# Seven products in place of eight for 18 of the second layer's 22 pairs of up-projection tiles, with neighbouring pairs interleaved

## The chip, the cores and the metric

The kernel runs on one core of a Trainium2 chip. The metric is the device time of one execution in microseconds (us); lower is better. Engines are named as the profile names them: PE (TensorE, matmuls), PEld (its weight loads), DVE (VectorE), ACT (ScalarE), POOL (GpSimd), SP (SyncE, which here only issues DMAs).

## What is computed

A two-layer encoder trunk runs over 768 tokens: 512 of a prompt and 256 of a sample, which share the weights but not the conditioning vector. Each layer has a mixer (attention and convolution) and then a gated feed-forward block (FFN). The change lies in the FFN of the second layer:

```python
D_MODEL = 1024
D_FF = 2816

def conv_ffn(h, w_up, dw_w, w_down):
    a, g = jnp.split(h @ w_up, 2, axis=-1)
    g = depthwise_conv(g, dw_w)          # width 3, centred, per request
    return (a * jax.nn.gelu(g)) @ w_down

def trunk(...):
    for l in range(DEPTH):
        ...
        h = rms_norm(x, norm2_g[l]) * (1 + s2) + sh2
        x = x + g2 * conv_ffn(h, w_up[l], ffn_dw_w[l], w_down[l])
```

## The kernel before

Everything lies transposed, 128 features on the partitions and 768 tokens along the free axis. The tokens form two groups, 512 and 256 wide (`GROUPS`). The precision comes from split numbers: a float32 value is kept as a high part `hi` (rounded) and a low part `lo` (the rest), and one product is three matmuls, `wl*xh`, `wh*xl`, `wh*xh` (`three`, L349 to L352).

Weights arrive as tiles of 128 x 1024 numbers (512 KB), eight blocks of 128 columns each. One list, `stream`, sets their order for the whole kernel. SP loads tile after tile into a ring of `RAW` = 5 buffers (L233); `consume` (L306) splits each one: ACT writes `wh` (L324), ACT writes `wl` = -raw (L328), and a DMA issued by POOL adds raw to it in place (L329), so that `wl` ends as raw minus its rounded part. The ring of split tiles has `PAIRS` = 4 places. `unit` hands the next split tile to a product.

The kernel is written in the order of a planner with its own clock: `tick` (L120) counts the matmuls' time, starts work that falls due (`after`), and lets `feed` (L332) split the next tile when at least 1.3 us of that clock have passed since the last and a place in the ring is free. The planner only sets the order in which instructions are written. On the chip every engine takes its own instructions in that order, and each instruction waits for what it reads and for the place that it writes.

The FFN of a layer (`ffn`, L856) works through 22 pairs f = 0 to 21. Pair f has two up-projection tiles, a and g, of 128 features each over all 1024 inputs: `product` (L358) runs 24 matmuls of 512 columns and 24 of 256 for each tile. `hidden` (L859) then makes the pair's hidden features: the convolution of g (ACT L865, DVE L866 and L867), GELU (ACT L868), the product with a (DVE L869), and the split of the result (ACT L870, POOL L871). The pairs are grouped by `CHUNKS` = (4, 4, 4, 4, 2, 4). `part` (L447) multiplies a finished group's hidden features by the down-projection, one weight tile per pair, and DVE adds the result to x (L445). It runs once per group, behind the first pair of the next group; the last two groups are multiplied at the end.

Names in what follows: `h_k` is the FFN's input (block k of 8, high and low), `a`, `g` the results of the two tiles in PSUM (eight banks), `gc` the hidden features on their way, `pd` the down-projection's results.

## Time and profile before

| | |
|---|---|
| median of 3 runs | 1901.63 us (1891.21 to 1901.82) |
| the profiled execution | 1892.81 us, of which the span from first to last instruction is 1891.0 us |
| mean granted TensorE clock | 0.991 of full speed |
| PE busy | 1840.4 us, 97% of the span |
| second layer's FFN | from about 1338 us to the end |

The page's first part gives each engine's busy time. Its slices (40 of them, 47.3 us each) show in tenths how busy an engine is along the span, and PEclk the clock that PE was granted. A row of the timeline has the start, the duration, the engine, the line and the operation with the tiles that it writes and reads; in brackets stands idle time in front of it and what ended it. Matmuls are pipelined, so that a matmul's time is the distance from its start to the next start, not its duration.

### The profile page before, as it was taken

What the parts mean: (1) busy time and instruction counts of PE and PEld (TensorE: products, weight loads), DVE (VectorE), ACT (ScalarE), POOL (GpSimd) and SP (SyncE); (2) the same over time, 40 slices, a digit from 0 to 9 for tenths busy, and PEclk for the clock granted to TensorE, in tenths of its full rate; (3) what the DMA queues carried; (4) which work ended last, traced back from release to release, by engine and by line L of the source; (5) the groups of instructions that cost most, each with busy time, mean ns of one, the idle gap of its engine ahead of it and who ended that gap; (6) DMA issues with size and microseconds to landing.
All of it is one profiled execution on the core that took longest, in us unless ns stands there. A gap on an engine that the chain in (4) does not pass through costs nothing.

```text
span 1891.0 us, 27649 instructions
## 1 busy us (share of the span) xinstructions
PE 1840.4 (97%) x11164; PEld 1552.1 (82%) x11164; DVE 1000.3 (53%) x1779; ACT 816.8 (43%) x1315; POOL 367.4 (19%) x344
## 2 busy tenths in 40 slices
PE   6999999999999999999999999999899999999999
PEld 4789676778888888888878986768788888888888
DVE  6667666776655655664367886666622221313123
ACT  3324667554423242433343357675543333333331
POOL 1103110033211121211232131100521121211110
PEclk9999999999999999999999999999999999999999
DMA  9666431236667777685635542223457464646454
GB/s 339 176 174 192 122 90 44 67 90 162 184 191 199 212 183 212 156 228 147 145 86 127 124 119 64 65 59 97 93 131 162 106 148 112 149 100 151 101 122 112
DMA packets 80913, 261.81 MB, mean 138 GB/s; under 512 B 9137, under 2 KB 18609, under 8 KB 80785
## 3 DMA queue, kind: packets, MB, share of 16 engines
q0 software_dynamic: 26640, 97.01, 28.4%
q1 hardware_dynamic: 54144, 163.03, 25.4%
q8 instruction: 88, 1.44, 0.3%
q14 instruction: 41, 0.33, 0.1%
HBM read 159.83 MB, written 3.18 MB: 86 GB/s over the span
## 4 chain that ended last, share of the span: by engine, by line
PE 90%; DVE 3%; ACT 2%; issue 2%; DMA 2%; POOL 1%; SPq 0%; POOLq 0%; ACTq 0%; DVEq 0%
PE a L351 6%; PE g L351 6%; PE g L352 6%; PE a L352 6%; PE a L350 6%; PE g L350 6%; PE pd L351 5%; PE pd L352 5%; PE pd L350 5%; PE s L729 4%; PE tp L763 2%; PE o L774 2%; PE v L350 1%; DMA wl<-raw 1%; PE q L350 1%
## 5 line engine op out<-in xcount | busy, mean ns | idle before, releaser
L329 POOL DMA_DIRECT2D wl<-raw x185 | 163.9, 886 | 691.1 <-ACT wl L328 498.0
L324 ACT ACTIVATE wh<-raw 128x1024 fp32r<-128x1024 f32 x188 | 197.2, 1049 | 163.4 <-PE pd L352 69.1
L866 DVE SCALAR_TENSOR_TENSOR gc<-g,fw_sb,gc 128x511 f32<-128x511 f32 x84 | 51.4, 612 | 389.6 <-ACT gc L865 389.6
L558 DVE SCALAR_TENSOR_TENSOR acc<-up,cw_sb,acc 128x783 f32<-128x783 f32 x240 | 246.8, 1028 | 4.3
L328 ACT ACTIVATE wl<-raw 128x1024 fp32r<-128x1024 f32 x185 | 193.4, 1046 | 0.0
L351 PE MATMUL pd<-hl,wh 128*128 128x512 f32 (+1 forms) x576 | 193.2, 335 | 0.0
L352 PE MATMUL pd<-hh,wh 128*128 128x512 f32 (+1 forms) x576 | 192.8, 335 | 0.0
L350 PE MATMUL pd<-hh,wl 128*128 128x512 f32 (+1 forms) x576 | 192.4, 334 | 0.0
L871 POOL TENSOR_TENSOR hl<-gc,hh 128x768 fp32r<-128x768 f32 x44 | 81.8, 1860 | 543.5 <-ACT hh L870 543.5
L865 ACT ACTIVATE gc<-g,fw_sb 128x512 f32<-128x512 f32 x84 | 48.2, 573 | 305.6 <-PE g L352 305.6
L292 DVE CUSTOM_DVE_ANT_0 cro<-raw,cr 128x1024 f32<-128x1024 f32 x112 | 166.6, 1488 | 4.2 <-ACT cr L285 1.5
L445 DVE SCALAR_TENSOR_TENSOR x<-pd,mod,x 128x512 f32<-128x512 f32 (+1 forms) x160 | 96.3, 615 | 133.9 <-PE pd L352 133.9
L350 PEld LDWEIGHTS pd<-hh,wl 128*128 128x128 f32 x576 | 108.1, 188 | 12.3
L351 PEld LDWEIGHTS pd<-hl,wh 128*128 128x128 f32 x576 | 108.3, 188 | 11.7
L352 PEld LDWEIGHTS pd<-hh,wh 128*128 128x128 f32 x576 | 108.2, 188 | 11.4
L868 ACT ACTIVATE gc<-gc 128x512 f32<-128x512 f32 x88 | 46.2, 525 | 130.1 <-DVE gc L867 130.1
L729 PE MATMUL s<-kT,qT 64*128 64x512 f32 (+1 forms) x192 | 94.1, 570 | 0.0
L869 DVE TENSOR_TENSOR gc<-a,gc 128x512 f32<-128x512 f32 x84 | 46.9, 558 | 55.0 <-ACT gc L868 55.0
L741 ACT ACTIVATE sp<-sp,nm 128x512 f32<-128x512 f32 (+1 forms) x96 | 62.1, 647 | 27.5 <-DVE nm L739 24.6
L739 DVE CUSTOM_DVE_ANT_0 sp<-s,G 128x512 f32<-128x512 f32 (+1 forms) x96 | 57.1, 596 | 24.0 <-PE s L729 24.0
L750 ACT ACTIVATE sp<-sp,den 128x512 f32<-128x512 f32 (+1 forms) x96 | 61.8, 645 | 9.0 <-DVE den L748 8.8
L764 ACT ACTIVATE PT<-tp 128x512 f32<-128x512 f32 (+1 forms) x96 | 49.3, 518 | 22.5 <-PE tp L763 21.9
(697 smaller groups left out, 5165.2 us busy)
## 6 DMA issues: line engine op xcount, KB each, us to landing
wl<-raw POOLq DMA_DIRECT2D x185, 512.0 KB, 5.8
raw<-in_w_up SPq DMA_DIRECT2D x88, 512.0 KB, 4.7
raw<-in_wadaT SPq DMA_DIRECT2D x48, 512.0 KB, 5.7
raw<-in_w_down SPq DMA_DIRECT2D x44, 512.0 KB, 4.5
raw<-in_w_in SPq DMA_DIRECT2D x40, 512.0 KB, 4.7
raw<-in_wada SPq DMA_DIRECT2D x24, 512.0 KB, 7.0
raw<-in_w_out SPq DMA_DIRECT2D x16, 512.0 KB, 4.7
G<-bt SPq DMA_DIRECT2D x16, 448.0 KB, 4.5
```

Of the source, the lines that this page charges most:

```text
L292: nc.vector.tensor_tensor_reduce(out=rows["out"], in0=r, in1=rows[g], op0=ALU.mult, op1=ALU.add, scale=1.0, scalar=0.0, accum_out=mod[l][: ...
L324: nc.scalar.activation(hi, r, AF.Copy)
L328: nc.scalar.activation(lo, r, AF.Copy, scale=-1.0)
L329: nc.gpsimd.dma_start(out=lo, in_=r, accum_op=ALU.add)
L350: nc.tensor.matmul(ps, wl, xh, start=first, stop=False)
L351: nc.tensor.matmul(ps, wh, xl, start=False, stop=False)
L352: nc.tensor.matmul(ps, wh, xh, start=False, stop=last)
L445: nc.vector.scalar_tensor_tensor(x[ot][:, span(g)], ps, mod[l][:, gate + ot, g:g + 1], x[ot][:, span(g)], op0=ALU.mult, op1=ALU.add)
L558: nc.vector.scalar_tensor_tensor(a, up[i][:, t:t + ACW], K["cw"][:, l, i, t:t + 1], a, op0=ALU.mult, op1=ALU.add)
L729: nc.tensor.matmul(ps[:, :w], qT[hp][64 * s:64 * s + 64, o + i * P:o + (i + 1) * P], kT[hp][64 * s:64 * s + 64, o:o + w], start=True, stop ...
L741: nc.scalar.activation(sp[:, :w], sp[:, :w], AF.Exp, scale=-1.0, bias=nm, accum_out=den)
L871: nc.gpsimd.tensor_tensor(lo, gc, hi.bitcast(F32), op=ALU.subtract)
```

## The change

For 18 pairs of the second layer (f = 4 to 21, all groups but the first, `SEVEN`), a pair's two up-projections become seven products of half size. The 1024 inputs are cut into two halves of four blocks, the tokens into two halves of 384 (`HALF`), and the pair's two tiles a and g are the two columns of a 2 x 2 arrangement of blocks. Strassen's scheme (in Winograd's form) then needs seven block products, each of four blocks and 384 tokens: 12 matmuls of 384 columns. The products take sums and differences as operands:

- Weights (a1, a2 the halves of tile a, g1, g2 those of tile g): A is tile a itself (split as before, its low part by the DMA); S holds g1+g2 and g1+g2-a1 (`sums`); B is g2 (`last_block`); R holds a1-g1 and a2-(g1+g2-a1) (`differences`). DVE computes S and R, ACT rounds them, and DVE makes the low parts of S, B and R (`split`), without a DMA.
- Tokens: four sets of sums t1 to t4, four blocks each, made once for the layer: t1 to t3 on DVE and ACT while pairs 1 to 3 run (`token_sums`, stepped by the planner), t4 in `last_sums` just ahead of pair 4, written over blocks of `h` that are not needed any more.

In PSUM, x, y and z (384 columns) collect the products of a pair; x and z are read on the way and added to further. A pair's own steps `first` to `last` are interleaved with those of the pair ahead, so that PE runs per pair, twelve matmuls each: x(n) from A(n); y(n-1) from B(n-1) and t4; y(n) from A(n); z(n-1) from R(n-1); x(n) on top from S(n) and t2; (here, in pairs 5, 9, 13 and 17, `part`); z(n) from S(n) and t1; x(n) on top from R(n) and t3. Besides, the rounding of each weight tile's low part is written 0.8 us of the planner's clock later (`whole`) in both layers, and raw tiles are counted until that point.

```diff
@@ constants
-ACT = 28
+ACT = 29
+HALF = NT // 2
+SEVEN = (6, 1)
+SUMS_FROM = (NF, 1)
+SUMS_RATE = (0.0, 1.1)
@@ layer_items
-                ff += [w_up[l, 2 * f], w_up[l, 2 * f + 1]]
...
+                if n < SEVEN[l]:
+                    ff += [("w", a) for a in ups]
+                else:
+                    ff += [("A", ups[0]), ("G", ups[1]), ("S", None)] + later + [("B", None), ("R", None)]
...
@@ load_ahead, consume
+            sums = any(a[0] in "AGSBR" for a in stream[state["item"]:len(loaded) + 1])
...
+            if state["raws"] >= min(most, RAW - sums):
+                return
...
+            {"w": whole, "A": first_block, "S": sums, "B": last_block, "R": differences}[it[0]](n, r, hi, lo)
+            ready.append((hi, lo, n))
...
+    def whole(n, r, hi, lo, freed=1):
         nc.scalar.activation(hi, r, AF.Copy)
...
-            nc.scalar.activation(lo, r, AF.Copy, scale=-1.0)
-            nc.gpsimd.dma_start(out=lo, in_=r, accum_op=ALU.add)
-        ready.append((hi, lo))
+            def low():
+                if n in open_low:
+                    open_low.remove(n)
+                    nc.scalar.activation(lo, r, AF.Copy, scale=-1.0)
+                    nc.gpsimd.dma_start(out=lo, in_=r, accum_op=ALU.add)
...
+            after(0.8, low)
+
+    def first_block(n, r, hi, lo):
+        held["a"] = r
+        whole(n, r, hi, lo, 0)
+
+    def split(hi, lo, r):
+        nc.scalar.activation(hi, r, AF.Copy)
+        nc.vector.tensor_tensor(lo, r, hi.bitcast(F32), op=ALU.subtract)
+
+    def sums(n, r, hi, lo):
...
+        nc.vector.tensor_tensor(s[:, :512], g[:, :512], g[:, 512:], op=ALU.add)
+        nc.vector.tensor_tensor(s[:, 512:], s[:, :512], a[:, :512], op=ALU.subtract)
+        split(hi, lo, s)
+
+    def last_block(n, r, hi, lo):
+
+        split(hi[:, :512], lo[:, :512], held["g"][:, 512:])
+
+    def differences(n, r, hi, lo):
+
+        a, g, s = held["a"], held["g"], held["s"]
+        nc.vector.tensor_tensor(g[:, :512], a[:, :512], g[:, :512], op=ALU.subtract)
+        nc.vector.tensor_tensor(g[:, 512:], a[:, 512:], s[:, 512:], op=ALU.subtract)
+        split(hi, lo, g)
@@ ffn: token sums
+        def token_sums():
...
+            for k in range(4):
+                t = yield from minus(column(k, 1), column(k, 0), f"s1{l}{k}")
+                keep(0, k, t)
...
+        def last_sums():
+
+            for k in range(4):
+                t, u = (tmp(f"{c}4{l}{k}", False)[:, :HALF] for c in "tu")
+                p, q, to = column(k + 4, 0), blocks[1, k], column(k, 1)
+                nc.vector.tensor_tensor(t, p[0].bitcast(F32), q[0].bitcast(F32), op=ALU.subtract)
+                nc.vector.tensor_tensor(u, p[1].bitcast(F32), q[1].bitcast(F32), op=ALU.subtract)
+                nc.vector.tensor_tensor(t, t, u, op=ALU.add)
+                nc.scalar.activation(to[0], t, AF.Copy)
+                nc.vector.tensor_tensor(to[1], t, to[0].bitcast(F32), op=ALU.subtract)
@@ ffn: one pair
+            def add(ps, u, half, xs, first):
+                for k in range(4):
+                    b = slice((4 * half + k) * P, (4 * half + k + 1) * P)
+                    for m, (p, q) in enumerate(((1, 0), (0, 1), (0, 0))):
+                        nc.tensor.matmul(ps, u[p][:, b], xs[k][q], start=first and k == 0 and m == 0, stop=k == 3 and m == 2,
+                                         skip_group_check=True)
...
+            def first():
...
+                add(o["x"], o["a"], 0, b11, True)
+                o["av"] = af(f"av{tag}")
+                S.activation(o["av"][:, left], o["x"], AF.Copy)
+
+            def second():
+                add(o["y"], o["a"], 1, b21, True)
+                release()
+                V.tensor_tensor(o["av"][:, left], o["y"], o["av"][:, left], op=ALU.add)
+
+            def third():
+                o["s"] = unit()
+                add(o["x"], o["s"], 1, t2, False)
+                S.activation(o["av"][:, right], o["x"], AF.Copy)
+
+            def fourth():
+                add(o["z"], o["s"], 0, t1, True)
+                release()
+                o["b"], o["r"] = unit(), unit()
+                add(o["x"], o["r"], 0, t3, False)
...
+                S.activation(o["gv"][:, left], o["x"], AF.Copy)
+                V.tensor_tensor(o["gv"][:, right], o["z"], o["gv"][:, left], op=ALU.add)
+
+            def fifth():
+                add(o["y"], o["b"], 0, t4, True)
+                release()
+                V.tensor_tensor(o["gv"][:, left], o["y"], o["gv"][:, left], op=ALU.add)
+                scaled(0)
+
+            def sixth():
+                S.activation(zs[0], zs[0], AF.Gelu_apprx_tanh)
+                scaled(1)
+                add(o["z"], o["r"], 1, b22, False)
...
@@ ffn: the loop over pairs
+            if n == SEVEN[l]:
...
+                last_sums()
...
+                    step[0]()
+                    if before:
+                        before[2][4]()
+                    step[1]()
+                    if before:
+                        before[2][5]()
+                    step[2]()
+                    if before:
+                        finish(*before[:2], before[2][6])
+                    step[3]()
+                    before = (n, i, step)
```

The place that matters most in a pair is ACT's order. First the kernel before, ACT from pair 6's gate to pair 7's (`gc1_6`, `gc1_7`: layer 1, pairs 6 and 7; wh142 to wh145: the next tiles):

```order
L865 ACTIVATE gc1_6_13569<-g1_6_00_13512,fw_sb_265 128x512
L868 ACTIVATE gc1_6_13569<-gc1_6_13569 128x512
L865 ACTIVATE gc1_6_13569<-g1_6_01_13544,fw_sb_265 128x256
L868 ACTIVATE gc1_6_13569<-gc1_6_13569 128x256
L870 ACTIVATE hh1_6_13570<-gc1_6_13569 128x768
L324 ACTIVATE wh142_13590<-raw222_13330 128x1024
L328 ACTIVATE wl142_13591<-raw222_13330 128x1024
L324 ACTIVATE wh143_13647<-raw223_13387 128x1024
L328 ACTIVATE wl143_13648<-raw223_13387 128x1024
L865 ACTIVATE gc1_7_13698<-g1_7_00_13641,fw_sb_265 128x512
```

The same engine after the change, pair 7 (wh148 is B of pair 7, wh149 its R, wh150 and wl150 A of pair 8, wh151 S of pair 8; gz the convolved gate of pair 6; L1065 reads x of pair 7 on the way):

```order
L1046 ACTIVATE gz1_60_13713<-gv1_6_13680,fw_sb_267 128x512
L386 ACTIVATE wh148_13720<-raw230_13507 128x512
L1083 ACTIVATE gz1_60_13713<-gz1_60_13713 128x512
L1046 ACTIVATE gz1_61_13735<-gv1_6_13680,fw_sb_267 128x256
L386 ACTIVATE wh149_13742<-raw230_13507 128x1024
L1088 ACTIVATE gz1_61_13735<-gz1_61_13735 128x256
L365 ACTIVATE wh150_13768<-raw234_13626 128x1024
L372 ACTIVATE wl150_13769<-raw234_13626 128x1024
L1065 ACTIVATE av1_7_13698<-x1_7_13683 128x384
L1094 ACTIVATE hh1_6_13783<-av1_6_13560 128x768
L386 ACTIVATE wh151_13802<-sum151_13804 128x1024
L1073 ACTIVATE gv1_7_13818<-x1_7_13683 128x384
```

The next pair's A tile (wh150, wl150) stands behind R of this pair (wh149), and the reading of x (L1065) behind both.

What wh149 reads is made on DVE. Its order in the same stretch after the change (gv the gate, av the a branch, raw230 tile g of pair 7, in which R is built in place):

```order
L1079 TENSOR_TENSOR gv1_6_13680<-y1_6_13546,gv1_6_13680 128x384
L1047 SCALAR_TENSOR_TENSOR gz1_60_13713<-gv1_6_13680,fw_sb_267,gz1_60_13713 128x511
L1048 SCALAR_TENSOR_TENSOR gz1_60_13713<-gv1_6_13680,fw_sb_267,gz1_60_13713 128x511
L387 TENSOR_TENSOR wl148_13721<-raw230_13507,wh148_13720 128x512
L1060 TENSOR_TENSOR av1_7_13698<-y1_7_13684,av1_7_13698 128x384
L1047 SCALAR_TENSOR_TENSOR gz1_61_13735<-gv1_6_13680,fw_sb_267,gz1_61_13735 128x255
L1048 SCALAR_TENSOR_TENSOR gz1_61_13735<-gv1_6_13680,fw_sb_267,gz1_61_13735 128x255
L405 TENSOR_TENSOR raw230_13507<-raw229_13505,raw230_13507 128x512
L406 TENSOR_TENSOR raw230_13507<-raw229_13505,sum147_13666 128x512
L387 TENSOR_TENSOR wl149_13743<-raw230_13507,wh149_13742 128x1024
```

R's two differences (L405, L406) stand behind the convolution of the pair ahead, whose first instruction (L1079) reads y after its last product.

The entry into the new scheme, ACT behind pair 3 (t410 to t413 are t4's four blocks, which DVE makes one behind the other; wh133 is R of pair 4; L1055 reads x of pair 4 for the first time):

```order
L951 ACTIVATE hh1_3_13021<-gc1_3_13020 128x768
L1017 ACTIVATE h11_0h_12236<-t410_13035 128x384
L1017 ACTIVATE h11_1h_12252<-t411_13042 128x384
L1017 ACTIVATE h11_2h_12273<-t412_13049 128x384
L1017 ACTIVATE h11_3h_12298<-t413_13056 128x384
L386 ACTIVATE wh133_13069<-raw211_12652 128x1024
L1055 ACTIVATE av1_4_13084<-x1_4_13063 128x384
L365 ACTIVATE wh134_13106<-raw215_12744 128x1024
```

The four roundings of t4, and R of pair 4, stand ahead of the first reading of pair 4's x.

## Rows read from the trace of the kernel before

**Rows 1.** The page: busy time by engine, then PE's busy tenths in 40 slices.

```profile
PE 1840.4 (97%) x11164; PEld 1552.1 (82%) x11164; DVE 1000.3 (53%) x1779; ACT 816.8 (43%) x1315; POOL 367.4 (19%) x344
PE   6999999999999999999999999999899999999999
```

**Rows 2.** Stretches: busy time of each engine, granted clock, DMA share; second FFN.

```profile
1500.00:1550.00 50.00, 50.00 (x296) 44.10 (x296) 13.64 (x23) 18.32 (x23) 10.03 (x10) 1.00 0.66 153
```

**Rows 3.** Timeline of PE in a product: 12 steps of 512 columns, then 23 of 256.

```profile
1594.16 0.40 PE L352 MATMUL a<-h_3h,wh 128*128 128x512 f32 x1
...
1596.91 0.39 PE L352 MATMUL a<-h_7h,wh 128*128 128x512 f32 x1
1597.14 0.28 PE L350 MATMUL a<-h_0h,wl 128*128 128x256 f32 x1
...
1599.75 0.28 PE L352 MATMUL a<-h_7h,wh 128*128 128x256 f32 x1
```

**Rows 4.** Timeline of ACT behind one pair.

```profile
1572.76 0.69 ACT L865 ACTIVATE gc<-g,fw_sb 128x512 f32<-128x512 f32 x1 [11.71 <-PE g L352]
1575.11 0.63 ACT L868 ACTIVATE gc<-gc 128x512 f32<-128x512 f32 x1 [1.66 <-DVE gc L867]
1575.65 0.46 ACT L865 ACTIVATE gc<-g,fw_sb 128x256 f32<-128x256 f32 x1
...
1578.44 0.85 ACT L870 ACTIVATE hh<-gc 128x768 fp32r<-128x768 f32 x1 [0.55 <-DVE gc L869]
1579.19 1.05 ACT L324 ACTIVATE wh<-raw 128x1024 fp32r<-128x1024 f32 x1
1580.14 1.04 ACT L328 ACTIVATE wl<-raw 128x1024 fp32r<-128x1024 f32 x1
```

**Rows 5.** Timeline of DVE behind the same pair.

```profile
1573.48 0.75 DVE L866 SCALAR_TENSOR_TENSOR gc<-g,fw_sb,gc 128x511 f32<-128x511 f32 x1 [14.01 <-ACT gc L865]
1574.27 0.75 DVE L867 SCALAR_TENSOR_TENSOR gc<-g,fw_sb,gc 128x511 f32<-128x511 f32 x1
1575.78 0.69 DVE L869 TENSOR_TENSOR gc<-a,gc 128x512 f32<-128x512 f32 x1 [0.76 <-ACT gc L868]
1576.39 0.47 DVE L866 SCALAR_TENSOR_TENSOR gc<-g,fw_sb,gc 128x255 f32<-128x255 f32 x1
...
1577.92 0.42 DVE L869 TENSOR_TENSOR gc<-a,gc 128x256 f32<-128x256 f32 x1 [0.54 <-ACT gc L868]
```

**Rows 6.** Timeline of POOL behind the same pair.

```profile
1579.37 1.85 POOL L871 TENSOR_TENSOR hl<-gc,hh 128x768 fp32r<-128x768 f32 x1 [17.06 <-ACT hh L870]
1581.59 0.87 POOL L329 DMA_DIRECT2D wl<-raw  x1 [0.36 <-ACT wl L328]
```

**Rows 7.** Tile wl from 1385 to 1840 us: issue to landing of its 56 DMAs.

```profile
DMA to landing us min/median/max: 4.5/5.6/9.8
```

**Rows 8.** The chain that ended last, ahead of the second FFN: start, us, what.

```profile
1330.41 0.96 ACT wl L328
...
1331.76 6.18 DMA wl<-raw
1338.08 0.73 PE u L350
```

**Rows 9.** First FFN's start: PE's timeline across a wait, then stretches behind it.

```profile
416.81 0.77 PE L350 MATMUL u<-h_0h,wl 128*128 128x512 f32 x1 [3.47 <-DMA wl<-raw]
417.37 0.63 PE L351 MATMUL u<-h_0l,wh 128*128 128x512 f32 x1
417.80 0.63 PE L352 MATMUL u<-h_0h,wh 128*128 128x512 f32 x1
...
416.80:420.30 3.50, 3.49 (x9) 2.79 (x10) 3.43 (x6) 1.57 (x3) 2.48 (x3) 0.55 0.53 153
```

**Rows 10.** DVE and POOL side by side at the second FFN's norm (timeline).

```profile
1328.79 1.13 DVE L402 TENSOR_TENSOR sq<-sq,sq 128x256 f32<-128x256 f32 x1
...
1328.06 1.58 POOL L440 TENSOR_TENSOR h_0l<-t,h_0h 128x512 fp32r<-128x512 f32 x1 [1.15 <-ACT h_0h L438]
```

**Rows 11.** Groups by line and shape: a DVE operation on two SBUF operands.

```profile
L593 DVE TENSOR_TENSOR ls<-ls,ls 128x512 f32<-128x512 f32 x6 | 4.1, 682 | 0.0
L593 DVE TENSOR_TENSOR ls<-ls,ls 128x256 f32<-128x256 f32 x6 | 2.5, 420 | 2.6 <-ACT ls L591 2.4
```

More of the change, by code (lines that the diff above doesn't have):

```diff
@@ L75, in af, with wide @@
         return act.tile([P, NT], F32, tag="act", name=name)
-    def wide(name, w):
-        return act.tile([P, w], F32, tag="wide", name=name, bufs=5)
+    def wide(name, w, kind=F32):
+        return act.tile([P, w], kind, tag="wide", name=name, bufs=5)
     def bank(name):
@@ L340, in unit @@
             consume()
-        return ready.pop(0)
+        u = ready.pop(0)
+        if u[2] in low_of:
+            low_of.pop(u[2])()
+        return u[:2]
     def release(n=1):
@@ L802, in mixer @@
         if l == 0:
-            us = [kslices(ready.pop(0)) for _ in range(3)]
+            us = [kslices(ready.pop(0)[:2]) for _ in range(3)]
             ada_first(1)
@@ L874, in ffn, with finish @@
         f = 0
         pend = []
+        hid = []
+        waiting = []
+        def finish(n, i, last):
+            nonlocal pend, hid
+            hid.append(last())
+            nk = CHUNKS[n]
+            if i == (nk if n == len(CHUNKS) - 1 else 1) - 1 and pend:
+                part(l, 40, pend, f"pd{l}_{n}")
+            if i == nk - 1:
+                pend, hid = hid, []
+        before = None
         for n, nk in enumerate(CHUNKS):
-            hold = nk if n == len(CHUNKS) - 1 else 1
@@ L878, in ffn @@
-            hid = []
+            if n == SEVEN[l]:
+                while conv_bg["gen"] is not None:
+                    conv_step(True)
+                last_sums()
             for i in range(nk):
-                if f == 0:
-                    us = [kslices(unit()) for _ in range(2)]
-                    a, g = product(us, hs, f"u{l}_{f}", key)
-                    release(2)
-                else:
-                    (a,) = product([kslices(unit())], hs, f"a{l}_{f}")
-                    release()
-                    (g,) = product([kslices(unit())], hs, f"g{l}_{f}")
-                    release()
-                hid.append(hidden(f, a, g))
+                if f == SUMS_FROM[l]:
+                    conv_bg.update(gen=token_sums(), rate=SUMS_RATE[l], acc=0.0)
+                if n >= SEVEN[l]:
+                    step = seven(f)
+                    step[0]()
[9 more added lines that the diff above has]
+                    before = (n, i, step)
+                else:
+                    if f == 0:
+                        us = [kslices(unit()) for _ in range(2)]
+                        a, g = product(us, hs, f"u{l}_{f}", key)
+                        release(2)
+                    else:
+                        (a,) = product([kslices(unit())], hs, f"a{l}_{f}")
+                        release()
+                        (g,) = product([kslices(unit())], hs, f"g{l}_{f}")
+                        release()
+                    finish(n, i, lambda: hidden(f, a, g))
@@ L890, in ffn @@
                 f += 1
-                if i == hold - 1 and pend:
-                    part(l, 40, pend, f"pd{l}_{n}")
-            pend = hid
+        if before:
+            before[2][4]()
+            before[2][5]()
+            finish(*before[:2], before[2][6])
         last_part(l, 40, pend, f"pe{l}", nxt)
```

151 lines of the change are left out of this document (129 added, 22 removed).

## The prediction

> **What bounds the kernel now.** I read the page's first part and slices first: PE is busy for 1840.4 of 1891.0 us, and in the slices from 1340 us on it stays at nine tenths throughout [rows 1]. Then the stretches of the second FFN: in 50 us PE is busy for 50.00 at the full granted clock, ACT for 18.32 and DVE for 13.64 [rows 2]. So PE alone sets the end there, and fewer matmul columns are worth their full time as long as PE never has to wait. The other engines have much spare time on average, but an average says nothing about a chain that runs through all of them. The last step was therefore to read from timelines how long each link of such a chain takes [rows 4 to 8].
>
> **What is removed.** Twelve starts of 512 columns lie 2.75 us apart, 0.229 us each, and 23 of 256 columns 2.61 us, 0.1135 us each [rows 3]. A tile costs 24 x (0.229 + 0.1135) = 8.22 us, a pair 16.44, 18 pairs 295.9 us. Both shapes come to 0.445 ns a column, so I take 0.171 us for 384 columns and 2.05 us for a product of twelve. Seven make 14.37 us, and 18 pairs 258.6. **Saved: 37.3 us**, if PE stays dense.
>
> **One pair, walked through the queues.** I place the durations of the rows in the order in which ACT and DVE now take their work, with 0 at x(n)'s first matmul, for a pair without `part`. DVE takes 0.69 us for 512 columns and 0.42 for 256 [rows 5, 11], so about 0.56 for 384; the convolution's instructions take 0.75 and 0.47, the second 0.79 behind the first; unrelated ones follow each other at 0.61 [rows 5]. ACT takes 0.63 for 512 columns, 0.54 to the next instruction, and 0.95 from one 1024-column instruction to the next [rows 4]. A hand-over between ACT and DVE costs 0.03 to 0.09 us (1572.76 + 0.69 to 1573.48) [rows 4, 5]; from PE to ACT I estimate 0.26 behind the last product's slot.
>
> - 0 to 4.10: x(n), then y(n-1). Only now is the gate of pair n-1 complete.
> - DVE adds y (4.36 to 4.92), ACT scales (to 5.58), DVE convolves 512 columns (to 7.15), then comes the low part of B (to 7.75), the addition to av (to 8.24), the convolution of 256 columns (to 9.25), and R's two differences (to 10.46).
> - ACT rounds R (10.55 to 11.60), does the second GELU (to 11.92), and only then takes A of the next pair: high part to 12.88, low part to 13.82.
> - POOL starts the DMA 0.41 us after ACT has ended (1581.18 to 1581.59) [rows 4, 6], and it lands 5.6 us later, in the best case 4.5 and in the worst 9.8 [rows 7]; PE starts 0.14 behind the landing (1331.76 + 6.18 to 1338.08) [rows 8]. So x(n+1), whose first matmul reads the low part, begins at **20.0 us** (18.9 with 4.5).
>
> The loop closes on itself, since the next gate again waits for two products behind this point. PE itself needs 14.37 us, and a pair took 16.44 before. On the way PE waits twice: x(n)'s last product has to wait until ACT has read x (L1065), which stands behind the next A in ACT's queue and ends at 14.3, while PE was ready at 12.3 (2.1 us); then 3.5 us for the DMA. S, with 2.6 us of DVE work behind this, is ready long before it is needed.
>
> Counting: of the 17 steps from one pair to the next, 12 are of this kind (6 to 7, 7 to 8, 8 to 9, the same behind 10 and 14, and 18 to 21). Each has 20.0 - 14.37 = 5.7 us of stall: 69 us.
>
> **Pairs with `part`** (5, 9, 13, 17). `part`'s first weight tile is on ACT right behind the 512-column scaling: high part 5.5 to 6.5, low part to 7.5, issued at 7.9, landed at 13.5. PE reaches `part` at 10.25, so it waits 3.4 us, four times: 14 us. Then `part` runs for 8 x 12 x 0.3425 = 32.9 us, and behind it B, R and the next A are split in time (A lands about 1 us before PE needs it): nothing more.
>
> **The entry at pair 4.** t4 can only be written when pair 3's last product has read `h`. Pair 3's convolution runs 5.6 us (1572.76 to 1578.34) [rows 4, 5], then t4 takes 1.65 us of DVE, 0.6 of ACT and 0.56 of DVE for each of four blocks, one behind the other because DVE waits for ACT: 11.4 us. R of pair 4 adds 1.3 on DVE and 1.0 on ACT, and then ACT reads x. That is 20.3 us behind pair 3, where PE has work for 4.1: 16.2 us of stall. The following A lands at 28.3, PE being ready at 26.4: another 1.9. At the end of the last pair the wait for L1065 comes once more, 2.1 us.
>
> **Hidden work.** t1 to t3 are 44 DVE operations, some 25 us, in pairs 1 to 3, whose PE time of 49 us covers them; uncovered they would cost a few us at the entry, where DVE has to be through with them. The later rounding of low parts costs nothing in the first 1330 us where PE has its next tile ready; where it waits for one, it is a shift of one ACT instruction (0.63 us at most). The low part of the hidden features on POOL (1.85 us [rows 6]) slows DVE's two-operand work beside it: a 256-column addition took 1.13 us beside POOL, not 0.42 [rows 10, 11]. In the pair it falls behind A's chain and is free; at the entry it adds about 1.5 us, kept for the range.
>
> **The sum.** 69 + 14 + 16.2 + 1.9 + 2.1 = 103 us of stalls, less 37.3 saved: +66 us.
>
> **The clock.** When PE had waited 3.47 us at the first FFN's start, the granted clock of the next 3.5 us was 0.55, which is 1.2 in place of 2.4 GHz for most of it, and 512-column matmuls started 0.43 us apart [rows 9] where 0.229 is usual [rows 3]. The waits here are as long (3.4 and 3.5 us), and x(n+1) and y(n), which lie in the loop, come right behind. A stretch of 3.5 us at half speed costs 1.75 us, and nothing when it falls on products outside the loop. I take 1.3 at 17 places: 22 us. By the Trainium skill ("TensorE: Matmul & The Clock Gate", section "Loop structure matters more than you think") bursts of matmuls with DMA waits between them run cold. These rows agree with it; without it the sum would be +66.
>
> That makes 1892.8 + 66 + 22 = **1980 us**, against the profiled execution's 1892.8 us, which lies 8.8 below the median of the runs shown and close to the fastest; the runs after may scatter by as much, which lies well within the range.
>
> One page would price the loop lower. The Trainium skill ("DMA: Bandwidth & Descriptors", section "Anatomy of one DMA — SWDGE (gpsimd) path") gives a fixed 2.0 us plus the bytes at 436 GB/s. For 512 KB that is an estimate of 3.2 us, so a pair would take 17.6 and the twelve 29 us less, which is still slower than before. The 56 landings here, 4.5 us at the least [rows 7], speak against it.
>
> **The rivals.**
> - *PE stays dense* (faster). The mechanism is the change's own: 37 us fewer matmul columns and no wait of note, 1856 us, or up to 1873 with the entry's 16 us. For it R's differences or the next A would have to come off this chain: the period has to fall from 20.0 to about 14.5. For it speaks only the spare time in the averages [rows 2]; against it the order of ACT, in which A stands behind R. Chance 0.09.
> - *The low parts come early and only ACT's queue binds*. With the DMA hidden, x(n)'s last product still waits for L1065, so that a pair takes 16.5 us, the same as before. Then 12 x 2.1 + 16 + 2 + 2 less 37.3 is +8, 1901 us. No landing so far was short enough, since even 4.5 us leaves 18.9. Chance 0.08.
> - *The clock stays low in the loop* (slower still). With a wait in every pair, x(n+1) and y(n) could run at half speed throughout: 4.1 us a pair, 2.8 more than I took, 12 times: 2014 us. Chance 0.10.
> - *The forecast*: 1980, by itself 1935 (landings of 4.5 us and no clock loss: 19 and 22 less) to 2005 (landings 1.2 us longer, the 1.5 us and some delay at the entry). Chance 0.73.
>
> **Range.** 1925 to 2025 takes in the forecast and the low clock, and leaves out the first two rivals. One per cent is about what a measurement of this kernel can tell from no change. Faster by more than that is the first rival (0.09, with a little for one that I don't see: 0.10), within it the second (0.08), slower the rest (0.82).
>
> **What would show it.** PE must have 216 matmuls fewer. Right: twelve pairs that lie about 20 us apart, each with a wait of x's first product for a DMA of wl (3 to 4 us) and one of its last for ACT L1065 (about 2 us); a wait of some 16 us at pair 4; four of 3.4 us at `pd`; granted clock near 0.5 behind the long ones. Wrong: pairs at 15 us or less, no wait for wl, or ACT ahead of PE because DVE's operations on 384 and 512 columns take far less than the rows say. If the waits are there but the clock holds, the time is near 1958.

## The result, and the profile after

| | median | range | ratio to the kernel before |
|---|---|---|---|
| changed kernel | 1990.4 us | 1978.27 to 1999.01, 4 runs | 1.048 [1.041, 1.055] |
| kernel before, beside it | 1900.6 us | 1891.21 to 1901.82, 4 runs | |

The change makes the kernel some 90 us slower. 1980 us were predicted, in a range of 1925 to 2025. The profiled execution took 1993.09 us; its span is 1991.3 us at a mean clock of 0.968.

The page of the changed kernel, lines that answer to [rows 1]: PE's busy time, its tenths and its clock in the 40 slices (49.8 us each), and the shares of the chain that ended last, then the same shares in the kernel before.

```profile
PE 1851.9 (93%) x10948; PEld 1585.0 (80%) x10948; DVE 1174.3 (59%) x2037; ACT 859.7 (43%) x1403; POOL 356.4 (18%) x326
PE   6999999989999999999999999999697888989889
PEclk9999999989999999999999999999799999999999
PE 75%; DVE 8%; DMA 6%; ACT 5%; issue 5%; POOL 1%; SPq 0%; ACTq 0%; DVEq 0%; POOLq 0%
...
PE 90%; DVE 3%; ACT 2%; issue 2%; DMA 2%; POOL 1%; SPq 0%; POOLq 0%; ACTq 0%; DVEq 0%
```

PE has 216 matmuls fewer, and yet 11.5 us more of busy time. A matmul at half the clock counts as busy for longer (some 34 us, see the sum below), which undoes what the missing ones save; and the tail of the last matmul ahead of each of the 36 waits counts as busy, too (6 us). From slice 28 on (1394 us, the first slice being 0) many nines have become sevens and eights, and a quarter of the chain runs through other engines than PE, where it was a tenth. What PE waited for, from 1400 us to the end (total, times, longest):

```profile
PE x L1028 <- DMA wl<-raw: 38.5, 16, 2.9
PE x L1028 <- ACT av L1065: 20.6, 12, 1.7
PE x L1028 <- ACT av L1055: 18.6, 1, 18.6
PE pd L431 <- DMA wl<-raw: 9.1, 5, 2.3
PE z L1028 <- DVE gv L1074: 1.8, 1, 1.8
PE x L1028 <- DVE wl L387: 0.5, 1, 0.5
```

The names are those of the prediction: x for the next A's transfer and for L1065 in every pair, the entry (L1055), `part` (pd). The loop itself can be read from the chain of one pair, from one landing to the next (start, us, what; pieces below 0.1 us and some of the convolution left out):

```profile
1516.25 4.49 DMA wl<-raw
...
1520.79 3.86 PE x L1028 x12
1524.65 2.09 PE y L1028 x12
...
1526.77 0.57 DVE gv L1079
...
1527.36 0.73 ACT gz L1046
...
1531.73 0.68 DVE raw L405
1532.42 0.61 DVE raw L406
...
1534.48 0.95 ACT wh L365
1535.42 0.95 ACT wl L372
1536.37 0.38 ACT av L1065
...
1536.78 4.54 DMA wl<-raw
...
1541.36 0.69 PE x L1028
```

A pair takes 1541.36 - 1520.79 = 20.57 us, and PE's own work is only two of its links. (L1065 stands in it by time: it fills the 0.4 us between ACT's second rounding and POOL's start, which lay there before the change too [rows 4, 6].) From x's first matmul to y's (1524.48) lie 3.69 us; at full clock twelve take 2.08. Two stretches of that pair (busy times, then PEclk):

```profile
1520.78:1524.94 4.16, 4.16 (x15) 4.16 (x16) 0.23 (x1) 0.26 (x1) 0.00 (x0) 0.60 0.02 4
1524.94:1541.36 16.42, 12.50 (x72) 11.87 (x70) 11.20 (x17) 8.43 (x13) 2.88 (x2) 0.99 0.36 96
```

Right behind the wait the granted clock is 0.60, as behind the one in [rows 9] it was 0.55; for the rest of the pair it is 0.99.

Eleven of the twelve such pairs take 20.52 to 20.64 us. One, from 1617.08, takes 22.42: there y ran at the low clock, too (0.50 over the first 4.12 us; the gate's addition starts 7.21 us behind x's first matmul, against 5.98 in the pair above), and A landed 5.2 us behind its issue. The 34 DMAs of wl from 1440 to 1940 us, those for `part` included:

```profile
DMA to landing us min/median/max: 4.5/4.6/8.4
```

**What is behind `part`.** ACT and PE at the end of `part` in pair 5 (timeline):

```profile
1493.23 1.06 ACT L365 ACTIVATE wh<-raw 128x1024 fp32r<-128x1024 f32 x1 [5.51 <-PE pd L433]
...
1500.23 0.69 PE L1028 MATMUL x<-h_0h,wl 128*128 128x384 f32 x1 [2.90 <-DMA wl<-raw]
```

ACT had nothing to do for 5.51 us and took the next A only when `part`'s last matmul had given its place back. PE then waited 2.90 us for it. The prediction had no wait here; it comes four times.

**The sum.** From pair 4's first matmul to the end the changed kernel took 577.8 us, the kernel before 480.0. The 18 pairs' columns at full clock are 295.9 - 18 x 7 x 12 x 0.1733 = 33.9 us fewer (384-column matmuls start 0.1733 us apart, at half the clock 0.320). Their matmuls took 32 us more than that, at the low clock. The gaps, each counted beyond a usual 0.17 us between two starts, are 95.0 us. The four runs of `part` and the last one took 4 us longer; 2 of these 4 us come without any wait in front (33.3 us a run, where the kernel before took 32.85). That is +97, and 2.6 us had been lost ahead of pair 4: 1891.0 + 97 + 2.6 = 1990.6, the span being 1991.3.

### The profile page after: what moved, and what is told of

Same layout as the page of the kernel before. It is cut to its first block, busy times and chain, and to the rows that moved or that the text cites. A ratio compares the mean times of both kernels' runs of the same rounds, so it can differ in the third digit from the quotient of the medians.

```text
span 1991.3 us, 27584 instructions
## 1 busy us (share of the span) xinstructions
PE 1851.9 (93%) x10948; PEld 1585.0 (80%) x10948; DVE 1174.3 (59%) x2037; ACT 859.7 (43%) x1403; POOL 356.4 (18%) x326
## 4 chain that ended last, share of the span: by engine, by line
PE 75%; DVE 8%; DMA 6%; ACT 5%; issue 5%; POOL 1%; SPq 0%; ACTq 0%; DVEq 0%; POOLq 0%
DMA wl<-raw 6%; PE pd L431 5%; PE pd L433 5%; PE pd L432 5%; PE s L810 4%; PE x L1028 3%; PE g L431 3%; PE a L431 3%; PE a L433 3%; PE g L433 3%; PE a L432 3%; PE g L432 3%; PE o L855 2%; PE tp L844 2%; PE y L1028 2%
## 5 line engine op out<-in xcount | busy, mean ns | idle before, releaser
L373 POOL DMA_DIRECT2D wl<-raw x167 | 147.2, 882 | 950.1 <-ACT wl L372 478.4
L365 ACT ACTIVATE wh<-raw 128x1024 fp32r<-128x1024 f32 x170 | 178.3, 1050 | 147.1 <-PE pd L433 51.8
L372 ACT ACTIVATE wl<-raw 128x1024 fp32r<-128x1024 f32 x167 | 174.7, 1046 | 0.0
L432 PEld LDWEIGHTS pd<-hl,wh 128*128 128x128 f32 x576 | 108.6, 188 | 12.3
L947 DVE SCALAR_TENSOR_TENSOR gc<-g,fw_sb,gc 128x511 f32<-128x511 f32 (+1 forms) x48 | 29.4, 612 | 137.6 <-ACT gc L946 137.6
L952 POOL TENSOR_TENSOR hl<-gc,hh 128x768 fp32r<-128x768 f32 x26 | 49.0, 1885 | 309.4 <-ACT hh L951 309.4
L946 ACT ACTIVATE gc<-g,fw_sb 128x512 f32<-128x512 f32 (+1 forms) x48 | 27.5, 572 | 154.6 <-PE g L433 154.6
L1028 PE MATMUL x<-ts,wl 128*128 128x384 f32 x144 | 50.7, 352 | 39.7 <-ACT av L1065 20.6
L1028 PE MATMUL x<-ts,wh 128*128 128x384 f32 x288 | 74.9, 341 | 0.0
L1079 DVE TENSOR_TENSOR gv<-y,gv 128x384 f32<-128x384 f32 x18 | 10.0, 558 | 105.3 <-PE y L1028 105.2
L386 ACT ACTIVATE wh<-raw 128x512 fp32r<-128x512 f32 (+1 forms) x36 | 30.3, 840 | 83.9 <-DVE raw L406 69.9
```

The costliest lines, as they stand in the source:

```text
L365: nc.scalar.activation(hi, r, AF.Copy)
L372: nc.scalar.activation(lo, r, AF.Copy, scale=-1.0)
L373: nc.gpsimd.dma_start(out=lo, in_=r, accum_op=ALU.add)
L432: nc.tensor.matmul(ps, wh, xl, start=False, stop=False)
L1028: nc.tensor.matmul(ps, u[p][:, b], xs[k][q], start=first and k == 0 and m == 0, stop=k == 3 and m == 2, skip_group_check=True)
```

## The experiments

The kernel before scattered from 1887.9 to 1902.7 us over thirteen runs. Pair 4 began between 1400.6 and 1415.9 us in the seven traces with seven products whose work up to there is nearly the same. Where a kernel ran once, I therefore compare by its trace, from the last matmul ahead of the entry's wait to the end of the span (below: **from the entry**). The changed kernel has 1991.3 - 1417.5 = 573.8 us there. How far this stretch scatters from run to run is not on record, since every kernel has one trace and the runs were on three chips; differences of a few us are therefore read pair by pair, not from the total. In the edits, `...` marks lines left out.

### The side edits alone

```diff
-SEVEN = (6, 1)
-SUMS_FROM = (NF, 1)
+SEVEN = (6, 6)
+SUMS_FROM = (NF, NF)
```

> All pairs by eight products as before the change, but with the change's side edits left in: the later rounding of low parts, raw tiles counted until then, the other constants. Theory (the whole loss comes from the pairs by seven products): like the kernel before, ratio 1.000 to 1.003, PE busy 1840 us with 11164 matmuls. Rival (the later rounding holds up the first layer, where the second FFN already began some 2 us later in the changed kernel's trace): 1.005 to 1.02 slower than before, with longer waits of PE for wl before 1340 us.

Measured: 1894.97 us beside 1897.6 of the kernel before, ratio 0.999 [0.996, 1.001], with 11164 matmuls. The later rounding of low parts and the new constants cost nothing that can be measured. The whole loss lies in the pairs by seven products and the work that goes with them.

### A's low part without a DMA

```diff
     def first_block(n, r, hi, lo):
         held["a"] = r
-        whole(n, r, hi, lo, 0)
+        split(hi, lo, r)
```

> One edit: the low part of tile A is made by DVE behind its high part, as those of S, B and R are, and no longer by ACT and a DMA. Theory (the loop that sets a pair's 20.55 us runs through the DMA that makes the next A's low part): ACT's second rounding (0.95 us), the hand-over to POOL (0.41) and the landing (4.5) go, a DVE operation of about 1.2 us comes, so a pair takes about 15.6 us, some 5 us less for 12 pairs; the half-clock stretches that followed the waits for the DMA shrink or go. PE's waits for a DMA of wl in front of x (38.5 us, 16 times) are gone, and so are the 3 us behind `part`. Total about 1908 us (1895 to 1925). Rival 1 (ACT's queue with the reading of x, L1065, sets the pair): the wait for L1065 stays or grows as the DMA's goes, a pair stays at 19 to 20 us, total near 1980. Rival 2 (384-column matmuls or the clock by themselves cost the time): period unchanged, total near 1990.

Measured: 1928.81 us, ratio 1.017 [1.0135, 1.0197], 519.3 us from the entry, 54.5 less. The DMA was the loop's last link, as said: PE's waits from 1395 us on have no row of x for a DMA any more, but that for L1065 has stayed.

```profile
PE x L1028 <- ACT av L1055: 19.8, 1, 19.8
PE x L1028 <- ACT av L1065: 19.4, 12, 2.2
PE pd L431 <- DMA wl<-raw: 12.8, 5, 3.5
```

The time is 20 us above what the theory gave, though. The first pair behind each `part` took 15.74 us, nearly the 15.6 expected; the other eight took 16.8 to 17.9, five of them 17.3 at full clock (PEclk, the third number from the end):

```profile
1505.73:1523.02 17.29, 15.08 (x85) 14.52 (x84) 13.79 (x19) 7.63 (x12) 1.81 (x2) 1.00 0.17 62
```

DVE and POOL in such a pair (timeline):

```profile
1522.89 2.36 DVE L394 TENSOR_TENSOR sum<-raw 128x512 f32<-128x512 f32 x1
1525.28 0.69 DVE L395 TENSOR_TENSOR sum<-sum,raw 128x512 f32<-128x512 f32 x1
...
1528.30 0.55 DVE L1074 TENSOR_TENSOR gv<-z,gv 128x384 f32<-128x384 f32 x1
1528.96 0.56 DVE L1079 TENSOR_TENSOR gv<-y,gv 128x384 f32<-128x384 f32 x1
...
1522.85 1.85 POOL L1095 TENSOR_TENSOR hl<-av,hh 128x768 fp32r<-128x768 f32 x1 [15.48 <-issue]
```

An addition of 512 columns that takes 0.69 us took 2.36 beside POOL's L1095. All that stands behind it in DVE's queue comes 1.7 us late. The gate's addition (L1079) comes late, too: the two products ahead of it had ended 4.2 us behind 1523.02, at 1527.2, and it began at 1528.96. By the Trainium skill ("SBUF — State Buffer", section "Who interferes with whom") a DVE instruction with two SBUF inputs contends with a GpSimd instruction that reads SBUF, and the port pair that they share is an exclusive lock. The trace agrees: POOL ends at 1524.70, DVE at 1525.25, 0.55 us later, where such an addition takes 0.69 alone.

These eight pairs make 14 of the 20 us. The waits at `pd` grew from 9.1 to 12.8 us, that at the entry from 18.6 to 19.8.

### The same, with POOL's work on DVE

```diff
-                nc.gpsimd.tensor_tensor(lo, o["av"], hi.bitcast(F32), op=ALU.subtract)
+                held["hl"] = lambda: V.tensor_tensor(lo, o["av"], hi.bitcast(F32), op=ALU.subtract)
...
@@ sums, behind S's rounding
+        held.pop("hl", lambda: None)()
...
```

> The run with A's low part on DVE, and one thing more: the low part of the hidden features (L1095, on POOL) is made by DVE, written behind the next S's rounding, where DVE waits for ACT. Theory (in that run a pair takes 17.3 us and not the 15.6 expected, because one of DVE's additions for S beside POOL's L1095 takes 2.2 to 2.4 us in place of 0.69, and the gate's addition stands behind it in DVE's queue): no DVE addition above 1.3 us in the pairs, a pair of 15.7 us, as the pairs right behind `part` already show; 12 pairs by 1.6 us, some 19 us less from the entry at pair 4 to the end (519 us there now, about 500 then). Rival (the 17.3 us come from ACT's queue up to the reading of x, L1065, by itself): 17.3 us as before or more, since DVE has 0.7 to 1 us more to do.

Measured: 500.2 us from the entry, 19.1 less than the run above (1908.44 us in all). Pairs take 15.7 to 15.9 us (one 16.1), the sums' additions 0.68 us each. The wait for the reading of x (L1070 here) is half of what it was. Below it stand one pair with PEclk and the moved subtraction (timeline):

```profile
PE x L1033 <- ACT av L1070: 9.5, 12, 1.0
...
1502.97:1518.82 15.85, 15.08 (x85) 14.50 (x85) 13.01 (x20) 7.64 (x12) 0.00 (x0) 1.00 0.19 67
...
1504.16 0.95 DVE L1101 TENSOR_TENSOR hl<-av,hh 128x768 fp32r<-128x768 f32 x1
```

The pairs became shorter because the additions no longer meet POOL; the 0.95 us that DVE does in its place stand where it would have waited for ACT. That 19 us were forecast and 19.1 measured is in part chance: 12 pairs by 1.6 us were counted, but four stood at 15.7 before. The other eight gave 11.9 us; the rest came in the stretches with `part` and at the end.

### x read ahead of A

```diff
             def third():
                 o["s"] = unit()
+                state["late"] = True      # feed() takes no A meanwhile
                 add(o["x"], o["s"], 1, t2, False)
                 S.activation(o["av"][:, right], o["x"], AF.Copy)
+                state["late"] = False
+                feed()
```

> One edit: the next A may be split only after ACT's reading of x (L1065) has been written, so that L1065 stands ahead of A's two roundings in ACT's queue; the low part's rounding falls behind that of the hidden features. Theory (the loop through A's DMA sets the pair, and the wait for L1065 lies inside time that is lost anyway): the waits for L1065 (20.6 us, 12 times 1.7) go, but A's low part starts about 2.4 us later, and a pair takes about 22.9 us in place of 20.55; the waits for wl grow from 2.9 to about 6 to 7 us; total about 2020 us. Rival (the reading of x in ACT's queue sets the pair): 1.7 us less a pair, total about 1972 us.

Measured: 2035.36 us, 617.6 from the entry, 43.8 more than the changed kernel. The waits for L1065 are gone, and a pair takes 23.6 to 24.9 us (22.9 expected). In the pair from 1528.21 (24.46 us) x and y ran 0.8 us longer at the low clock than in the changed kernel, and POOL issued A's DMA 0.7 us later, since its own subtraction for the hidden features (1546.21 to 1548.17) now stood ahead of it. PE's waits:

```profile
PE x L1030 <- DMA wl<-raw: 94.1, 17, 7.1
```

So the wait for L1065 cost nothing by itself: it lay inside time that was lost to the loop anyway. What counts is when A's second rounding stands in ACT's queue.

### One DVE operation more in the loop

```diff
         split(hi[:, :512], lo[:, :512], held["g"][:, 512:])
+        nc.vector.tensor_tensor(lo[:, :512], held["g"][:, 512:], hi[:, :512].bitcast(F32), op=ALU.subtract)
```

> One addition: DVE computes the low part of B a second time, a 512-column operation of 0.6 to 0.7 us that stands in DVE's queue between the 512-column and the 256-column convolution, ahead of R's differences. Theory (DVE's queue up to R's differences is a link of the loop): every pair becomes longer by just that, 20.55 to about 21.2 us, 12 times, total 8 us more than the changed kernel, about 2000 us. Rival (DVE has slack there, the loop runs through something else): period 20.55 as before and total unchanged, near 1992 us.

Measured: 570.7 us from the entry, 3.1 less than without the addition, where 8 more were expected. The first three pairs take 20.92, 19.61 and 21.18 us; the mean of all twelve is 20.41, against 20.72 in the changed kernel. Four stretches with PEclk, two of x's last product and two of x's first:

```profile
1504.99:1508.50 3.51, 3.51 (x11) 3.51 (x12) 2.29 (x4) 1.90 (x2) 2.90 (x2) 0.53 0.81 182
1509.51:1513.70 4.19, 4.19 (x24) 4.19 (x25) 0.51 (x1) 0.49 (x1) 0.00 (x0) 1.00 0.02 4
1524.56:1527.31 2.75, 2.75 (x12) 2.75 (x12) 1.53 (x4) 1.91 (x2) 2.42 (x2) 0.71 0.71 173
1529.11:1532.80 3.69, 3.69 (x12) 3.69 (x13) 0.19 (x1) 0.00 (x0) 0.00 (x0) 0.54 0.00 0
```

In the pair from 1509.51 the low clock had fallen on the last product of x ahead of it, whose delay the wait for the DMA swallowed, and the loop's own products ran at 1.00: 19.61 us. In the pair from 1529.11 they ran at 0.54: 21.18. At like clock in the loop the operation does cost what it takes: 21.18 against 20.57 at half, and 19.61 against 18.92 at full clock (the run that comes last but one). The total can't show it, since the operation also moved the stretches of low clock.

### t4's sums ahead of time

```diff
@@ constants
-SUMS_RATE = (0.0, 1.1)
+SUMS_RATE = (0.0, 1.35)
@@ token_sums, behind t2
...
+                nc.vector.tensor_tensor(u, p[0].bitcast(F32), u, op=ALU.subtract)
+                nc.vector.tensor_tensor(u, u, p[1].bitcast(F32), op=ALU.add)
+                fourth_sums.append(u)
...
@@ last_sums
-                nc.vector.tensor_tensor(t, p[0].bitcast(F32), q[0].bitcast(F32), op=ALU.subtract)
-                nc.vector.tensor_tensor(u, p[1].bitcast(F32), q[1].bitcast(F32), op=ALU.subtract)
-                nc.vector.tensor_tensor(t, t, u, op=ALU.add)
+                t, to = fourth_sums[k], column(k, 1)
@@ the loop over pairs, pair 4
-                last_sums()                # sums, rounding and low parts, ahead of pair 4
...
+                    step[1]()
+                    last_sums()            # rounding and low parts, behind its product for y
```

> The changed kernel with t4's sums made during pairs 1 to 3, from t2's values before their split (8 DVE operations fewer than 12, spread over the pairs); ahead of pair 4 nothing of t4 is left, and its roundings and low parts are written behind pair 4's product for y, once x has been read. Theory (t4's chain of DVE and ACT, one block behind the other, is most of the entry's wait): the wait of x's second product for L1055 falls from 18.6 us to 6 to 9, which pair 3's convolution (5.6 us), R of pair 4 and the reading of x leave; about 11 us less from the entry to the end, pairs unchanged at 20.5 us. Rival (the wait is that of R and the roundings of the tiles, and t4 lies beside it): 16 us or more remain.

Measured: 561.5 us from the entry, 12.3 less, and the entry's wait is 8.9 us:

```profile
PE x L1031 <- ACT av L1058: 8.9, 1, 8.9
```

Nine of the pairs stay at 20.5 to 21.1 us; three take 19.0 to 19.1, with full clock in the loop. A wait of 2.1 us for the next A appeared, and, ahead of the entry, 1.6 in pair 3 for DVE. So pair 4 itself is 8.4 us shorter; the rest of the 12.3 lies behind it. In the changed kernel the first of t4's four chains had met POOL (timeline; the same addition takes 0.56 us in the other three):

```profile
1422.14 2.20 DVE L1016 TENSOR_TENSOR t<-t,u 128x384 f32<-128x384 f32 x1
...
1422.12 1.80 POOL L952 TENSOR_TENSOR hl<-gc,hh 128x768 fp32r<-128x768 f32 x1 [10.14 <-ACT hh L951]
```

### `part`'s first tile without a DMA

```diff
-                    later = [("w", w_down[l, u0 + q]) for q in range(pend)]
+                    later = [("w" if q or n < SEVEN[l] else "D", w_down[l, u0 + q]) for q in range(pend)]
@@ consume: "D" is split by split(), its low part by DVE
```

> The changed kernel, but the first weight tile of `part` (pairs 5, 9, 13, 17) has its low part made by DVE without a DMA. Theory (PE waits at `part` for that tile's DMA, 2.2 us each): the waits of pd for wl go from 9.1 us to below 1, four times 2.2 us less, 9 us from the entry to the end; the pairs without `part` and the 3 us behind `part` stay. Rival (PE would wait there anyway for what stands around it): pd waits for something else by about as long, 0 to 2 us less in all.

Measured: 558.0 us from the entry, 15.8 less; pd waits for nothing any more. The gaps are 11.2 us fewer, 9.9 of them those of pd (each counted, as above, beyond 0.17 us). `part` itself is 2.0 us shorter, since no low clock follows a wait there (33.29 us in all four runs; the longest took 34.97), and the pairs' matmuls lost 2.6 us less to the clock.

### A ahead of R and B, behind `part` only

```diff
@@ layer_items (owed: the tiles of `part` that follow the pair ahead)
-                    ff += [("A", ups[0]), ("G", ups[1]), ("S", None)] + later + [("B", None), ("R", None)]
-                    later = []
+                    ab = [("A", ups[0]), ("G", ups[1])]
+                    if owed:
+                        ff += owed + ab + [("R", None), ("B", None), ("S", None)]
+                    else:
+                        ff += ([] if owed is None else [("B", None), ("R", None)]) + ab + [("S", None)]
+                    owed, later = later, []
...
@@ differences: in a's raw tile
-        nc.vector.tensor_tensor(g[:, :512], a[:, :512], g[:, :512], op=ALU.subtract)
-        nc.vector.tensor_tensor(g[:, 512:], a[:, 512:], s[:, 512:], op=ALU.subtract)
-        split(hi, lo, g)
+        nc.vector.tensor_tensor(a[:, :512], a[:, :512], g[:, :512], op=ALU.subtract)
+        nc.vector.tensor_tensor(a[:, 512:], a[:, 512:], s[:, 512:], op=ALU.subtract)
+        split(hi, lo, a)
```

> The changed kernel, but behind `part` alone A of the next pair takes its place in the ring ahead of R and B of this pair, so that it is split while `part` still runs (R is built in a's raw tile and B comes last; in the pairs without `part` the order of the rings is as it was). Theory (the 3 us that x waits behind each `part` come from the ring: B and R take the two free places, and A can be written only when `part` has given back its last weight tile): the four waits of x for wl behind `part` go, at most a wait of below 1 us for R takes their place; 4 times 3 us and the half-clock stretches behind them, 12 to 18 us less from the entry at pair 4 to the end (574 us there now); the twelve other pairs keep 20.5 us and their waits. Rival (A is late there for its transfer or for the raw tile's load): about 3 us remain behind each `part`.

Measured: 553.5 us from the entry, 20.3 less (12 to 18 expected). Sixteen waits for A have become twelve, and nothing has taken their place. Below them stands the first pair behind `part`, with PEclk:

```profile
PE x L1038 <- DMA wl<-raw: 27.3, 12, 3.2
...
1498.03:1516.93 18.90, 15.05 (x85) 14.41 (x84) 12.84 (x19) 9.22 (x15) 2.92 (x2) 1.00 0.30 83
```

The run differs in one thing more: it may load one raw tile further ahead. That this was the cause is ruled out by the changed kernel's trace. At all four places ACT's wait for A there (5.51, 5.53, 5.53 and 5.40 us) ended with PE's last matmul of `part`, not with a load.

The gaps are 11.6 us fewer, and the matmuls lost 9.6 us less to the clock: of the four first pairs behind `part` three took 18.9 us, just what the walk through the queues gives for a landing of 4.5 us. Their loop began without a wait, and at full clock. The fourth took 20.0, since the next A came 1.1 us later.

### All of it at once, with A ahead of R in every pair

```diff
@@ layer_items: the next A and G ahead of R and B, in every pair
+                    ab = [("A", ups[0]), ("G", ups[1])]
+                    ff += ab + [("S", None)] if owed is None else owed + ab + [("R", None), ("B", None), ("S", None)]
+                    owed, later = later, []
...
@@ fifth: gate, S's low part, A of the next pair, convolution
...
                 V.tensor_tensor(o["gv"][:, left], o["y"], o["gv"][:, left], op=ALU.add)
-                scaled(0)
+                scale(0)
+                flush()
+                place("DAG")
+                convolve(0)
+                flush()
@@ sixth: R, 256-column convolution, R's low part
                 add(o["z"], o["r"], 1, b22, False)
                 release()
+                place("R")
+                convolve(1)
+                flush()
...
@@ hidden of pair 3: R of pair 4, its first product and the reading of x in the middle
+                if mid and g == 0:
+                    place("AGR")
+                    mid()
...
```

(`place` splits the next tiles of the stream, `flush` writes the DVE low parts that were held back.)

> The seven products in another order of the work around them. A of the next pair is split one pair earlier, ahead of B and R of this pair; R is built in a's raw tile, ahead of the 256-column convolution; x's reading (L1107 here) stands right behind R's rounding; DVE's low parts are written one step later, where DVE would wait for ACT; the hidden features' low part is made on DVE; t4's sums come in pairs 1 to 3, and the first tile of `part` has its low part from DVE. Theory (the loss is all a matter of the chain through DVE, ACT and the DMA, and the 34 us of removed columns are real): a pair takes 14.6 us, PE waits only at the entry (below 5 us) and at the end (2 to 4 us), the clock stays at 1.00, and the time is 1855 to 1885, likeliest 1866, ratio 0.98 to 0.99 to the kernel before. Rival 1 (DVE with 13 us of work a pair, in order and with its waits for ACT, becomes the bound): a pair takes 15.5 to 17 us, 1885 to 1910. Rival 2 (the clock or the columns cost by themselves): pairs above 17 us or half clock without waits, above 1910.

Measured: 1868.97 us (1865.02 to 1872.26), ratio 0.988 [0.984, 0.991]. This is faster than both kernels, than the kernel before by 1.2%. A pair takes 14.59 to 14.61 us in all twelve cases. All waits of PE from 1380 us to the end, and one pair with PEclk:

```profile
PE x L1067 <- ACT av L1097: 4.7, 1, 4.7
PE z L1067 <- DVE gv L1118: 2.0, 1, 2.0
PE a L463 <- DVE s L1035: 0.8, 1, 0.8
...
1500.11:1514.71 14.60, 14.60 (x86) 14.60 (x86) 11.76 (x19) 8.70 (x13) 0.88 (x1) 1.00 0.42 107
```

PE has no wait in a pair, the clock holds, and A still comes by the same DMA, which lands in time because it starts earlier:

```profile
1505.69 1.04 ACT L371 ACTIVATE wh<-raw 128x1024 fp32r<-128x1024 f32 x1
1506.65 1.05 ACT L378 ACTIVATE wl<-raw 128x1024 fp32r<-128x1024 f32 x1
...
1509.37 1.06 ACT L393 ACTIVATE wh<-raw 128x1024 fp32r<-128x1024 f32 x1 [0.76 <-DVE raw L420]
1510.73 0.49 ACT L1107 ACTIVATE av<-x 128x384 f32<-128x384 f32 x1 [0.30 <-PE x L1067]
...
1508.10 0.88 POOL L379 DMA_DIRECT2D wl<-raw  x1 [13.73 <-ACT gz L1084]
```

A (L371, L378) now stands ahead of R (L393), and the reading of x (L1107) follows R at once and waits only for PE. The changed kernel had R, A, reading. (What the expectation calls one pair earlier is this: counted from x's first matmul, A's first rounding starts at 5.6 us, and in the changed kernel at 13.6.) Which of the run's other edits the pairs need is not shown. So the scheme's 34 us are real. Some 24 were kept (the kernel before took 1893.3 us beside it). The three waits above, 7.5 us, and some 5 us of low clock behind that of the entry account for the rest, within the scatter of the runs.

## Why the prediction was right, and where it was not

- **The loop through A's DMA: right.** Two products, gate, convolution, R, ACT with A behind R, DMA, x: the chain above has the links in the order of the walk. Taking the DMA out shortened it at once (from 20.57 to between 15.7 and 17.9 us), putting A further back lengthened it (24), and in the last run, which changed more besides, putting it ahead of R dissolved it (14.6).
- **The period's terms.** The walk gave 20.0 us, 21.3 with the clock's 1.3, and 20.57 were measured. Two sizes were off, in opposite ways. The landing took 4.5 us in the pairs, not 5.6, and the minimum of [rows 7] was the value to take. Its median is from a stretch in which the DMA engines were busy to 0.66 [rows 2], here to 0.36; that the traffic makes the difference is likely, but no run changed it alone. The clock took 1.6 us in a pair, not 1.3. With 4.5 us the walk gives 18.9, and pairs at full clock took 18.9 to 19.1. By the Trainium skill ("DMA: Bandwidth & Descriptors", section "Anatomy of one DMA — SWDGE (gpsimd) path") the estimate was 3.2 us; the 4.49 and 4.54 of the chain decide against it.
- **The waits in the pair.** 2.1 and 3.5 us were predicted, 1.9 and 2.35 measured from start to start; twelve pairs lost 51 us, not 69. The shorter landing accounts for most of that. The wait for L1065 is a part of the loop's loss and costs nothing on top, as the walk had it: the run that removed it got slower.
- **The step that failed: "behind it B, R and the next A are split in time (A lands about 1 us before PE needs it): nothing more".** It cost 12.3 us of gaps (four times 3.07) and the clock behind them. I had walked the queues there but not the ring: S and `part`'s last weight tile hold two places, B and R take the other two, and A has to wait for `part`'s end. Giving A its place before B gave back 20.3 us.
- **`part`'s first tile:** 2.2 us a time instead of 3.4, again the landing. Its removal gave back 15.8 us, more than the 9.9 of the waits; 4.6 of the rest are the clock.
- **The entry:** 18.8 us instead of 16.2. Most of the difference is DVE's third operation for t4, which took 2.20 us beside POOL's L952 in place of 0.56 (the rows stand with the run of t4's sums). That was named and left out of the sum ("about 1.5 us, kept for the range"). The 1.9 us for the A that follows did not come.
- **Saved columns:** 33.9 us instead of 37.3, since 384 columns take 0.1733 us and not 0.171. **The clock:** 34 us (32 in the pairs, 2 in `part`) instead of 22.
- **The end:** 3.6 us in three waits instead of 2.1 in one.
- **Two slips in its sums:** 12 x (20.0 - 14.37) is 67.6, not 69, and 1980 less 19 and 22 is 1939, not 1935. Neither moves the range.

The stalls came to 95 instead of 103 us, with 12 us at a place where none was expected and 18 fewer in the loop; the clock and the columns added 15. Another 2.6 us were lost ahead of pair 4. So the time came out 10 us above the predicted one. That it came so near is in part luck, since errors of 12 to 18 us have both signs. It was no rival's time: PE did not stay dense, A's landing never came early enough, and the clock stayed low for the whole of the loop in one pair of the twelve.

Still open: which waits bring the low clock, and how far it then reaches. The runs show where it fell, but no run set it.

## What to carry to other kernels

Before fewer columns are counted as time, follow one round of the new loop through every in-order queue and every ring, and compare its length with PE's own work. Here 14.6 us of matmuls stood against 19 us of a chain that ended in the next round's weights. The cure was another order more than a faster link: what the next round needs goes ahead of what this round needs late, and DVE gets work to do where it would wait for ACT. Behind `part` little but the order was changed, and the wait went; the run with 14.6 us a pair changed several things at once.

## What the runs showed of the hardware

- DVE's additions of two SBUF operands beside a POOL subtraction took 2.36 us for 0.69 (512 columns) and 2.20 for 0.56 (384), and everything behind them in the queue shifted by that. Doing POOL's 1.9 us on DVE took 0.95 us there and was the better bargain.
- The low clock follows some waits and not others. Two waits per pair, of 1.7 and 2.2 us with 2.1 us of matmuls between them, were followed by 0.60 over the next 4.2 us. One wait of 2.2 us per pair left 1.00 over the whole pair in five pairs of seven and 0.96 in two (A's low part on DVE); one of 0.8 to 1.0 us left 1.00 in all twelve (the hidden features' low part on DVE, too).
- Where the low clock falls matters as much as how long it lasts. On a product that waits behind it anyway it cost nothing; on the two products of the loop 1.6 us. So an operation of 0.7 us added to the loop did not make the kernel slower.
